# Tokens and their forms moved 96 bytes from the weight rings, and a causal mask read as a repeated view

## The chip, the cores and the metric

The kernel runs on one core of a Trainium2 chip. The metric is the device time of one execution in microseconds (us), here as the median of several runs. The engines are TensorE (PE, whose weight loads the profile lists as PEld), VectorE (DVE), ScalarE (ACT), GpSimd (POOL) and SyncE (SP), which issues most DMAs.

## What is computed

A decoder trunk of two layers for 512 tokens of width 1024, in float32 inputs and outputs. Each layer is a feed-forward block, a token mixer with four memory heads beside it, and another feed-forward block, each followed by a layer norm over a scaled residual. The mixer of layer 0 is latent attention (MLA), that of layer 1 sparse attention (NSA), whose keys and values come from the tokens after layer 0.

```python
def swiglu(x, w_gu, w_down):
    g, u = jnp.split(x @ w_gu, 2, axis=-1)
    return (jax.nn.silu(g) * u) @ w_down

for layer in range(DEPTH):                                  # DEPTH = 2
    x = layer_norm(DN_ALPHA * x + 0.5 * swiglu(x, ffn_w_gu[layer, 0], ffn_w_down[layer, 0]), ...)
    if layer < N_A_LAYERS:
        o_tok, q_mem = mla_mix(x, ...)                      # 12 heads, causal
    else:
        o_tok, q_mem = nsa_mix(x, ...)                      # compressed, selected and window keys, causal
    o_mem = memory_attention(q_mem, mem, w_mem_kv[layer])
    x = layer_norm(DN_ALPHA * x + jnp.concatenate([o_tok, o_mem], -1) @ w_out[layer], ...)
    x = layer_norm(DN_ALPHA * x + 0.5 * swiglu(x, ffn_w_gu[layer, 1], ffn_w_down[layer, 1]), ...)
    if layer == N_A_LAYERS - 1:
        shared = nsa_shared_kv(x, ...)
```

The hidden width is 2816, that is 22 blocks of 128.

## The kernel before

**Products in three parts.** Every operand of a large product is kept as two float32r tiles, a rounded part (hi) and the rest (lo), and a product is hi·hi + hi·lo + lo·hi. `split` makes the two: ScalarE rounds (L198), VectorE subtracts (L199).

**Weights.** A fixed list, `_unit_order`, names every weight unit of [128, 1024] floats in the order of use. `prep` loads a unit by a DMA on SP's queue into one of four `wraw` buffers and splits it into a pair `whi`, `wlo`. The pairs lie in a ring of three (`wring`) and, inside the feed-forward stages, also in an extension of four (`W.extra`, the pool `wx`). `ahead` runs up to four units before the use.

**Feed-forward.** The gate and up products have the weights stationary and the tokens streamed, feature-major. Of the 22 blocks some ("s") are computed directly by `feature_major` (L352, L354 and L357: whi with xhi, whi with xlo, wlo with xhi), the others ("d") by a scheme with seven quarter products in place of eight, `seven`, whose quarters stream 256 columns on L365, L366 and L369:

```python
        for k in range(4):
            ks = slice(off + k * P, off + (k + 1) * P)
            nc.tensor.matmul(ps, lhsT=hi[:, ks], rhs=xh[:, k], start=k == 0, stop=False)
            nc.tensor.matmul(ps, lhsT=hi[:, ks], rhs=xl[:, k], start=False, stop=False)
        for k in range(4):
            ks = slice(off + k * P, off + (k + 1) * P)
            nc.tensor.matmul(ps, lhsT=lo[:, ks], rhs=xh[:, k], start=False, stop=k == 3)
```

Here `xh`, `xl` are either cut views of the token tiles `xhi`, `xlo` ([128, 8, 512]) or combinations of their quarters, the forms `t` ([128, 4, 256] each), which `token_forms` makes once for each block from plain copies `b`. The down product and the output product of the mixer have the hidden tiles (`hhi`, `hlo`) or the mixed heads (`mix`) stationary and 512 columns of weights streamed: `prod`, L400 to L405.

**Other products named below.** The gate and memory-query projection of layer 1 (`gates_qmem`, by `mm3`, L344 to L346) keeps token tiles stationary, for each of four token tiles, and streams 292 columns of weights for each of eight k; three of these chunks lie one behind the other in a unit, at 0, 1168 and 2336 bytes. The compressed keys (also `mm3`) have 64 stationary columns (`zh`) under 256 streamed ones. In the NSA heads a causal mask is added to the scores by a bf16 matmul of the identity with a mask (L1137); there the mask stands twice, for selected and window keys, in 256 columns.

**Memory.** SBUF is handed out from both ends. On the left stand, in order: 4 KiB of descriptors and 128 bytes of small constants, the pool `const` (`cst` [128, 416] float32 and `cbf` [128, 384] bfloat16, 2432 bytes of a partition), `wraw`, `wring`, and then pools that come and go by stage. A feed-forward stage opens (`open_f`) `xp` (residual x0 to x3, norm gains `g`, `b`, and xhi, xlo), then `wx`, then `sm` and `fm` (the forms). Between the feed-forward stages this room holds the heads' tiles, in layer 1 the keys `ke`, `ko` and values first, then queries, `ptc` (transposed block scores) and scores. `hhi`, `hlo`, `mix` and `zh` come from the right end. There a 96-byte tile `rest` stands in the pool of statistics. All the tiles that matmuls read start on a multiple of 64 bytes.

**Order.** Each engine runs its instructions in order; SP's queue too. A tile that lies on room of an older tile waits until that one's last reader is done. After a mixer, `out_proj` reloads the residual tiles x0 to x3 that were spilled to HBM (L1213) and runs the output product; `residual` (L308) adds a tile's product, `norm_tile` norms it.

Of the kernel before, what the change touches and what calls it, by code (L numbers as in the profile page):

```python
# [9 lines left out]
F32 = mybir.dt.float32  # L10
F32R = mybir.dt.float32r
BF16 = mybir.dt.bfloat16
# [5 lines left out]
P = 128  # L18
# [12 lines left out]
NRAW, NRING, NEXTRA = 4, 3, 4  # L31
# [72 lines left out]
def tile_trunk(ctx: ExitStack, tc, a: dict, out):  # L104
    nc = tc.nc
    order = _unit_order()

    const = ctx.enter_context(tc.tile_pool(name="const", bufs=1))
# [8 lines left out]
    class W:  # L117
        pos = 0
        done = 0
        scope = None  # L120
# [84 lines left out]
    def zero(t):  # L205
        nc.vector.memset(t.bitcast(F32), 0.0)

    cst = const.tile([P, 416], F32, name="cst")
    nc.gpsimd.dma_start(cst[:, 0:400], a["cst"])
    ident = cst[:, 0:128]  # L210
    valid = cst[:, 384:385]
    cbf = const.tile([P, 384], BF16, name="cbf")
    identb = cbf[:, 0:128]
    maskb = cbf[:, 128:256]
    maskb2 = cbf[:, 128:384]
    mhalf = cst[:, 385:387]

    class F:
# [22 lines left out]
    def stat(tag, bufs):  # L241

        return small.tile([P, 2, 4], F32, tag=tag, name=tag, bufs=bufs)
# [7 lines left out]
    def s2tile():  # L251
        return PS.left.tile([P, 1024], F32, tag="s2", name="s2", bufs=2)

    def s1tile():
        return PS.left.tile([P, 512], F32, tag="s1", name="s1")
# [6 lines left out]

    def open_f(scope):
        F.st = ExitStack()
        F.xp = F.st.enter_context(tc.tile_pool(name=f"xp{scope}", bufs=1, reuse_waits="tile"))
        W.extra = F.st.enter_context(tc.tile_pool(name=f"wx{scope}", bufs=NEXTRA, reuse_waits="tile"))
        F.sm = F.st.enter_context(tc.tile_pool(name=f"sm{scope}", bufs=2, reuse_waits="tile"))
        F.x = [F.xp.tile([P, D], F32, name=f"x{t}") for t in range(NT)]
        F.bk = 0
        W.scope = scope  # L270
        W.count = 0
        F.fst = ExitStack()
        F.fm = F.fst.enter_context(tc.tile_pool(name=f"fm{scope}", bufs=1, reuse_waits="tile"))
# [291 lines left out]
    def memory_pool():  # L565
        M.st, M.mp = right_pool("memp")
# [529 lines left out]
    def nsa_heads(gt, qf):  # L1096
# [18 lines left out]
        def weigh(rs, gi):  # L1115

            nc.vector.scalar_tensor_tensor(rs, rs, 1e-30, gi, op0=ALU.max, op1=ALU.mult)
            nc.vector.reciprocal(rs, rs)

        def head(u):  # L1120
            nm, rs = (stat(e, 3).rearrange("p a (b r) -> p (a b) r", r=2) for e in ("nm", "rs"))
            pp = hp.tile([P, 2560], F32, tag="p", name="pp", bufs=5)
            pbuf[u] = pp
            pr, par = divmod(u, 2)
            h = pr + 6 * par
            qt = F.qx[pr % 2][par]
            kt = (S.ke, S.ko)[par]
            for i in (3, 2, 1, 0):
                s = s1tile() if i == 1 else s2tile()
                q = slice(i * P, (i + 1) * P)  # L1130
                n = (i + 1) * P
                for c0 in range(0, 2 * n, 512):
                    c1 = min(c0 + 512, 2 * n)
                    for x in range(2):
                        nc.tensor.matmul(s[:, c0:c1], lhsT=qt[:, x, q], rhs=kt[:, x, c0:c1],  # L1135
                                         start=x == 0, stop=x == 1 and c1 < 2 * n)
                nc.tensor.matmul(s[:, 2 * n - 256:2 * n], lhsT=identb, rhs=maskb2, start=False, stop=True)  # L1137
                sv = s[:, 0:2 * n].rearrange("p (b r k) -> p r b k", r=2, k=P)
                po = pp[:, 2 * P_OFF[i]:2 * P_OFF[i] + 2 * n].rearrange("p (r b k) -> p r b k", r=2, k=P)
                nc.vector.tensor_reduce(nm[:, i], sv, axis=AX.XY, op=ALU.max, negate=True)  # L1140
                for r in range(2):
                    nc.scalar.activation(po[:, r], sv[:, r], AF.Exp,
                                         bias=nm[:, i, r:r + 1], accum_out=rs[:, i, r:r + 1])
                if i in (2, 0):
                    weigh(rs[:, i // 2 * 2:i // 2 * 2 + 2], gt[:, i // 2 * 2:i // 2 * 2 + 2, 3 * h + 1:3 * h + 3])
                    for ii in (i // 2 * 2, i // 2 * 2 + 1):
                        n = (ii + 1) * P
                        po = pp[:, 2 * P_OFF[ii]:2 * P_OFF[ii] + 2 * n].rearrange("p (r k) -> p r k", r=2)
                        nc.gpsimd.tensor_tensor(po, po, rs[:, ii, :, None].to_broadcast([P, 2, n]), op=ALU.mult)
                yield  # L1150
# [24 lines left out]
        def scores():  # L1175
            for u in range(HEADS):
                yield from head(u)
# [50 lines left out]
    for side in ("left", "right"):  # L1228
        psum_pool(side, "f0")
    open_f(0)  # L1230
    new_xt()
    new_blocks()
# [16 lines left out]
                prep()  # L1249
    sst.close()  # L1250
    nc.vector.tensor_copy(cbf[:, 0:256], cst[:, 0:256])
    nc.vector.tensor_copy(cbf[:, 256:384], cst[:, 128:256])
    memory_pool()

    def load_x():
# [17 lines left out]
    ast.close()  # L1273
    shared_pool()
    open_f(1)
    out_proj(0)
    mst.close()
# [18 lines left out]
    ast.close()  # L1296
    S.st.close()
    open_f(2)
    out_proj(1)
    mst.close()  # L1300
# [154 lines left out]
```

## Time and profile before

| | us |
|---|---|
| median of 3 runs | 1921.31 (1921.25 to 1922.46) |
| the profiled execution | 1921.12 |
| its span in the profile | 1919.2 |
| PE busy, PEld busy | 1888.3, 1686.0 |
| DVE, ACT, POOL busy | 1470.2, 870.1, 164.4 |

The profile records one execution. Busy time counts the stretches in which an engine has at least one instruction under way; matmuls overlap, so the distance between the starts of two that follow each other tells more than their durations. Times in its rows are us from the start of the span, mean durations in groups are ns. L198 is line 198 of the kernel.

### The profile page before, as it was taken

To read this page: it belongs to the slowest core of one execution; us is meant where nothing else is said; L and a number is where in the kernel's file an instruction comes from. 1 tells how busy PE (TensorE), PEld (TensorE's weight loads), DVE (VectorE), ACT (ScalarE), POOL (GpSimd) and SP (SyncE) were. 2 spreads that over 40 slices of the span, in tenths; PEclk is the share of its full clock that TensorE was granted. 3 is DMA by queue.
4 is the path that set the end of the run, shared out by engine and by line. 5 is a ranking of instruction groups with operands and counts; after the bars stand their busy time and mean duration, and the time that the engine had idled before them with its cause. 6 is when DMAs were issued, how large, how long until landed. Compare 5 with 4: busy or idle time off the path is not lost.

```text
span 1919.2 us, 31480 instructions
## 1 busy us (share of the span) xinstructions
PE 1888.3 (98%) x12560; PEld 1686.0 (88%) x12560; DVE 1470.2 (77%) x2363; ACT 870.1 (45%) x1435; POOL 164.4 (9%) x185
## 2 busy tenths in 40 slices
PE   9999999999999999999999999999999999999998
PEld 8999999886679999999989999998856689999997
DVE  7788788757658779778787987977477477887886
ACT  5344344446545335334653433444466344434432
POOL 0000000025400000000100000001255200000000
PEclk9999999999999999999999999999999999999999
DMA  6333334530133234234333323334321324323322
GB/s 235 110 110 101 119 99 147 175 100 34 45 121 129 81 100 132 77 100 143 120 112 110 121 87 100 121 105 160 110 45 27 101 75 132 101 87 110 111 79 75
DMA packets 59715, 203.88 MB, mean 106 GB/s; under 512 B 6945, under 2 KB 7217, under 8 KB 59569
## 3 DMA queue, kind: packets, MB, share of 16 engines
q1 hardware_dynamic: 57136, 194.70, 31.2%
q0 software_dynamic: 2432, 7.17, 1.3%
q8 instruction: 99, 1.62, 0.4%
q14 instruction: 48, 0.39, 0.1%
HBM read 188.21 MB, written 7.34 MB: 102 GB/s over the span
## 4 chain that ended last, share of the span: by engine, by line
PE 91%; DVE 3%; ACT 2%; issue 1%; POOL 1%; DMA 1%; POOLq 0%; DVEq 0%; ACTq 0%
PE bank L366 14%; PE bank L369 13%; PE bank L365 13%; PE bank L404 4%; PE bank L402 4%; PE bank L401 4%; PE bank L400 4%; PE bank L403 4%; PE bank L405 4%; PE bank L357 3%; PE bank L354 3%; PE bank L352 3%; PE o L633 3%; PE tb L605 3%; PE s L1135 1%; PE bank L346 1%
## 5 line engine op out<-in xcount | busy, mean ns | idle before, releaser
L198 ACT CAST whi<-wraw 128x1024 fp32r<-128x1024 f32 (+3 forms) x479 | 463.0, 974 | 593.5 <-PE bank L405 255.9
L199 DVE TENSOR_TENSOR wlo<-wraw,whi 128x1024 fp32r<-128x1024 f32 (+3 forms) x479 | 536.5, 1126 | 138.5 <-ACT whi L198 129.8
L366 PE MATMUL bank<-t,whi 128*128 128x256 f32 x1232 | 309.1, 284 | 0.0
L365 PE MATMUL bank<-t,whi 128*128 128x256 f32 x1232 | 309.0, 283 | 0.0
L366 PEld LDWEIGHTS bank<-t,whi 128*128 128x128 f32 x1232 | 237.0, 192 | 0.0
L365 PEld LDWEIGHTS bank<-t,whi 128*128 128x128 f32 x1232 | 236.8, 192 | 0.0
L366 PE MATMUL bank<-xlo,whi 128*128 128x256 f32 x924 | 231.8, 284 | 0.0
L365 PE MATMUL bank<-xhi,whi 128*128 128x256 f32 x924 | 231.7, 283 | 0.0
L369 PE MATMUL bank<-t,wlo 128*128 128x256 f32 x1232 | 198.3, 284 | 0.0
L366 PEld LDWEIGHTS bank<-xlo,whi 128*128 128x128 f32 x924 | 177.7, 192 | 0.7
L365 PEld LDWEIGHTS bank<-xhi,whi 128*128 128x128 f32 x924 | 177.4, 192 | 0.7
L369 PEld LDWEIGHTS bank<-t,wlo 128*128 128x128 f32 x1232 | 170.1, 192 | 0.0
L308 DVE SCALAR_TENSOR_TENSOR x<-x,bank 128x512 f32<-128x512 f32 x176 | 112.6, 682 | 68.2 <-PE bank L404 65.4
L369 PE MATMUL bank<-xhi,wlo 128*128 128x256 f32 x924 | 148.7, 284 | 0.0
L403 PE MATMUL bank<-wlo,hhi 128*128 128x512 f32 x336 | 131.3, 391 | 0.0
L401 PE MATMUL bank<-whi,hhi 128*128 128x512 f32 x336 | 131.2, 390 | 0.0
L404 PE MATMUL bank<-whi,hlo 128*128 128x512 f32 x336 | 131.1, 390 | 0.0
L405 PE MATMUL bank<-whi,hlo 128*128 128x512 f32 x336 | 131.0, 390 | 0.0
L400 PE MATMUL bank<-whi,hhi 128*128 128x512 f32 x336 | 130.9, 390 | 0.0
L402 PE MATMUL bank<-wlo,hhi 128*128 128x512 f32 x336 | 130.9, 390 | 0.0
L352 PE MATMUL bank<-xhi,whi 128*128 128x256 f32 (+1 forms) x472 | 129.5, 305 | 1.3 <-ACT xhi L198 1.3
L354 PE MATMUL bank<-xlo,whi 128*128 128x256 f32 (+1 forms) x472 | 129.4, 305 | 0.9 <-DVE xlo L199 0.9
(331 smaller groups left out, 3532.9 us busy)
## 6 DMA issues: line engine op xcount, KB each, us to landing
wraw<-in_gu SPq DMA_DIRECT2D x175, 512.0 KB, 3.4
wraw<-in_dn SPq DMA_DIRECT2D x88, 512.0 KB, 3.9
wraw<-in_wo SPq DMA_DIRECT2D x16, 512.0 KB, 3.6
wraw<-in_wm SPq DMA_DIRECT2D x8, 512.0 KB, 4.3
x_dram<-x SPq DMA_DIRECT2D x8, 512.0 KB, 2.9
x<-x_dram SPq DMA_DIRECT2D x8, 512.0 KB, 4.1
wraw<-in_w SPq DMA_DIRECT2D x8, 512.0 KB, 4.4
wraw<-in_wq SPq DMA_DIRECT2D x6, 512.0 KB, 3.7
```

The costliest lines, as they stand in the source:

```text
L198: nc.scalar.copy(hi, src)
L199: eng.tensor_tensor(lo, src, hi.bitcast(F32), op=ALU.subtract)
L352: nc.tensor.matmul(ps[:, c0:c1], lhsT=hi[:, k * P:(k + 1) * P], rhs=F.xhi[:, k, c0:c1], start=k == 0, stop=False)
L365: nc.tensor.matmul(ps, lhsT=hi[:, ks], rhs=xh[:, k], start=k == 0, stop=False)
L366: nc.tensor.matmul(ps, lhsT=hi[:, ks], rhs=xl[:, k], start=False, stop=False)
L369: nc.tensor.matmul(ps, lhsT=lo[:, ks], rhs=xh[:, k], start=False, stop=k == 3)
L400: nc.tensor.matmul(p0, lhsT=ahi, rhs=hi[:, 0:512], start=first, stop=False)
L401: nc.tensor.matmul(p1, lhsT=ahi, rhs=hi[:, 512:1024], start=first, stop=False)
L402: nc.tensor.matmul(p0, lhsT=ahi, rhs=lo[:, 0:512], start=False, stop=False)
L403: nc.tensor.matmul(p1, lhsT=ahi, rhs=lo[:, 512:1024], start=False, stop=False)
L404: nc.tensor.matmul(p0, lhsT=alo, rhs=hi[:, 0:512], start=False, stop=last)
L405: nc.tensor.matmul(p1, lhsT=alo, rhs=hi[:, 512:1024], start=False, stop=last)
```

## The change

It shortens `cst` to the 400 columns that are used, and drops the second copy of the mask in `cbf` with the copy that filled it. `const` is then 2112 bytes of a partition, 320 less, and `wraw` and `wring` start 320 bytes earlier. The mask matmul of the NSA heads reads the one mask through a view that repeats it. In a feed-forward stage `wx` is opened ahead of `xp`, and `xp` begins with a tile of 24 floats, 96 bytes, that nothing reads or writes. So both weight rings stay on the 64-byte grid, and x0 to x3, g, b, xhi, xlo, the forms and their copies start 32 bytes off it.

```diff
-    cst = const.tile([P, 416], F32, name="cst")
+    cst = const.tile([P, 400], F32, name="cst")
     nc.gpsimd.dma_start(cst[:, 0:400], a["cst"])
...
-    cbf = const.tile([P, 384], BF16, name="cbf")
+    cbf = const.tile([P, 256], BF16, name="cbf")
     identb = cbf[:, 0:128]
     maskb = cbf[:, 128:256]
-    maskb2 = cbf[:, 128:384]
...
     def open_f(scope):
         F.st = ExitStack()
+        W.extra = F.st.enter_context(tc.tile_pool(name=f"wx{scope}", bufs=NEXTRA, reuse_waits="tile"))
         F.xp = F.st.enter_context(tc.tile_pool(name=f"xp{scope}", bufs=1, reuse_waits="tile"))
-        W.extra = F.st.enter_context(tc.tile_pool(name=f"wx{scope}", bufs=NEXTRA, reuse_waits="tile"))
+        F.xp.tile([P, 24], F32, name="offset")
...
-                nc.tensor.matmul(s[:, 2 * n - 256:2 * n], lhsT=identb, rhs=maskb2, start=False, stop=True)
+                nc.tensor.matmul(s[:, 2 * n - 256:2 * n], lhsT=identb, rhs=maskb[:, None, :].to_broadcast([P, 2, P]), start=False, stop=True)
...
     nc.vector.tensor_copy(cbf[:, 0:256], cst[:, 0:256])
-    nc.vector.tensor_copy(cbf[:, 256:384], cst[:, 128:256])
```

## Rows read from the trace of the kernel before

**Rows 1.** Busy time of each engine; granted PE clock in 40 slices (tenths).

```profile
PE 1888.3 (98%) x12560; PEld 1686.0 (88%) x12560; DVE 1470.2 (77%) x2363; ACT 870.1 (45%) x1435; POOL 164.4 (9%) x185
...
PEclk9999999999999999999999999999999999999999
```

**Rows 2.** The chain that ended last, by engine.

```profile
PE 91%; DVE 3%; ACT 2%; issue 1%; POOL 1%; DMA 1%; POOLq 0%; DVEq 0%; ACTq 0%
```

**Rows 3.** Groups by form: count, busy us, mean ns.

```profile
L365 PE MATMUL bank<-t,whi 128*128 128x256 f32 x1232 | 309.0, 283 | 0.0
...
L365 PE MATMUL bank<-xhi,whi 128*128 128x256 f32 x924 | 231.7, 283 | 0.0
...
L400 PE MATMUL bank<-whi,hhi 128*128 128x512 f32 x336 | 130.9, 390 | 0.0
...
L352 PE MATMUL bank<-xhi,whi 128*128 128x256 f32 x400 | 99.8, 286 | 1.3 <-ACT xhi L198 1.3
```

**Rows 4.** Timeline of PE, quarter products: start us, duration us; twelve starts apart.

```profile
200.57 0.28 PE L365 MATMUL bank<-t,whi 128*128 128x256 f32 x1
...
202.01 0.28 PE L365 MATMUL bank<-t,whi 128*128 128x256 f32 x1
```

**Rows 5.** Timeline of PE, output product of layer 0; twelve starts apart.

```profile
546.43 0.39 PE L400 MATMUL bank<-whi,mix 128*128 128x512 f32 x1
...
549.15 0.39 PE L400 MATMUL bank<-whi,mix 128*128 128x512 f32 x1
```

**Rows 6.** Timeline of PE, compressed keys; twelve starts apart.

```profile
965.97 0.28 PE L344 MATMUL bank<-whi,zh 128*64 128x256 f32 x1
...
967.33 0.28 PE L344 MATMUL bank<-whi,zh 128*64 128x256 f32 x1
```

**Rows 7.** Timeline of PE, gate projection of layer 1, second token tile.

```profile
1331.60 0.30 PE L344 MATMUL bank<-whi,xhi 128*128 128x292 f32 x1
...
1332.40 0.30 PE L344 MATMUL bank<-whi,xhi 128*128 128x292 f32 x1
...
1332.81 0.29 PE L344 MATMUL bank<-whi,xhi 128*128 128x292 f32 x1
...
1333.20 0.30 PE L344 MATMUL bank<-whi,xhi 128*128 128x292 f32 x1
...
1334.81 0.30 PE L344 MATMUL bank<-whi,xhi 128*128 128x292 f32 x1
```

**Rows 8.** Timeline of PE, start of layer 0's second feed-forward block.

```profile
585.73 0.28 PE L352 MATMUL bank<-xhi,whi 128*128 128x256 f32 x1
...
586.44 1.12 PE L357 MATMUL bank<-xhi,wlo 128*128 128x256 f32 x8
587.40 0.28 PE L352 MATMUL bank<-xhi,whi 128*128 128x256 f32 x1
...
588.00 0.28 PE L354 MATMUL bank<-xlo,whi 128*128 128x256 f32 x1
```

**Rows 9.** Layer 1's heads end: SP, PE, DVE timelines; a window's busy, clock, DMA.

```profile
1488.86 9.61 SPq L1213 DMA_DIRECT2D x<-x_dram  x4
1528.21 0.33 SPq L129 DMA_DIRECT2D wraw<-in_wo  x1
...
1524.22 1.13 PE L1164 MATMUL o<-ptc,svc 128*128 128x512 f32 x2
...
1539.79 0.69 DVE L308 SCALAR_TENSOR_TENSOR x<-x,bank 128x512 f32<-128x512 f32 x1 [1.73 <-PE bank L404]
...
1520.00:1540.00 20.00, 19.99 (x89) 14.47 (x88) 9.86 (x10) 8.52 (x10) 1.14 (x2) 1.00 0.64 203
```

**Rows 10.** Mask matmuls and second mask copy: duration ns min/median/max.

```profile
L1137 PE MATMUL s<-cbf x48: 272/284/287, 1390.5 to 1497.3; 128*128 128x256 bf16 x48
...
L1252 DVE CAST cbf<-cst x1: 219/219/219, 6.8 to 6.8; 128x128 bf16<-128x128 f32 x1
```

## The prediction

> **What bounds the kernel now.** The page's busy row comes first: PE is busy for 98% of the span, at a granted clock of nine tenths or more in every slice, and the chain that ended last is 91% PE [rows 1, 2]. So the time is a count of matmuls times the distance from one start to the next, and a change of layout matters where it changes that distance. This is not the mean in the groups (283 ns and more), which overlaps the next matmul; it comes from the starts in the timeline.
>
> The groups by form give the counts [rows 3]: with the token tiles and their forms (xhi, xlo, t) as the streamed operand there are 1232 + 924 = 2156 matmuls of 256 columns on L365, as many on each of L366 and L369, and 400 on each of L352, L354 and L357: 6468 + 1200 = 7668. The timeline shows twelve of them in 202.01 - 200.57 = 1.44 us, 120.0 ns each [rows 4]. At 2.4 GHz, the level that the clock stands at here, 256 columns take 106.7 ns: each loses 13.3 ns. The output and down projections, 512 columns with the weights streamed, lose the same: 549.15 - 546.43 = 2.72 us for twelve, 226.7 ns against 213.3 [rows 5]. Where only 64 stationary columns are loaded, twelve streams of 256 take 1.36 us, 113.3 ns each: half the loss [rows 6]. So the loss goes with the load of the next weights that runs under the stream; the two meet somewhere. This is what 32 bytes could change: 7668 x 120.0 ns = 920 us, 48% of the span, of which 102 us are loss.
>
> The Trainium skill says on the page TensorE: Matmul & The Clock Gate (Part 2, step by step) that PE has two independent SBUF read ports, so that loading the next weights takes no read bandwidth from the running matmul. The trace does not bear this out here: 120.0 ns with 128 stationary columns, 113.3 with 64.
>
> **The change part by part.** *Tokens 32 bytes off the grid.* Before, streamed and stationary operands all start on the 64-byte grid. After, const is 320 bytes shorter, so the rings move by 320 and stay on the grid, and xhi, xlo and t stand 96 bytes further than they, off it. No row shows a 256-column stream so placed. Two rows come near.
>
> The first is the gate projection in layer 1: 292 columns of streamed weights, in chunks of 292 floats, so that of each three chunks the first starts on the grid, the second 16 bytes off and the third 32 off, under stationary tokens that stay on it. One chunk is three matmuls from one L344 start to the next [rows 7]. The third chunk takes 1332.81 - 1332.40 = 0.41 us, the next, on the grid again, 0.39; starts are read to 10 ns, so this is 136.7 against 130.0 ns with 5 of doubt. The whole token tile, eight chunks of mixed place, takes 1334.81 - 1331.60 = 3.21 us for 24 matmuls, 133.8 ns: a loss of 12.1 over 121.7. A stream that doesn't always start in step thus loses 12.1 instead of 13.3, which is -1.2 ns.
>
> The second is what the 256-column matmuls themselves do just after a disturbance: from 585.73 to 586.44 six take 0.71 us, 118.3 ns each, and a microsecond on (587.40 to 588.00) five take 0.60, 120.0 again [rows 8]. So 120.0 is no floor; it is a state that the stream falls into, with both operands on the grid. One that starts half a grid step later need not fall into it: -1.7 ns.
>
> I take the first, since it includes shifted operands in a steady stream: 7668 x 1.2 = -9.2 us. Bounds: below, the loss halves as with 64 stationary columns, -6.7 ns or -51 us; above, the costliest chunk (136.7 ns, loss 15.0) gives +1.7 ns or +13 us, and the step from rows 6 to rows 4, taken once more, +6.7 ns or +51.
>
> The Trainium skill has SBUF lines of 16 bytes (SBUF — State Buffer, Door 1, the note on cachelines). By that rule 32 bytes are two whole lines, and the term would be 0 instead of -9.2 us. The trace doesn't decide it: the means of chunks in different places differ by hardly more than their starts are read to.
>
> *Rings against the tiles that stay.* hhi, hlo and mix stay where they are, the rings move by 320 bytes; both remain on the 64-byte grid. Stationary tiles at steps of 256 bytes show one distance throughout [rows 6]. I take 0; 1 ns either way on the 6 x 336 matmuls of the down projection would be 2 us [rows 3].
>
> *Pools exchanged.* With the ring extension ahead of the tokens, tiles cover other old tiles at a change of stage. In layer 1, x0 to x3 lay over ke and ko, and their four loads went out from 1488.86 to 1498.47, while the heads still ran. After, x0 and x1 lie over ptc, which L1164 reads last at 1524.22 for 1.1 us, so that all four (2 MB) go out at about 1525.4. SP works in order; behind them stand the last wo load (1528.21) and the next gate weights. Their issue isn't later, since the wo load waits for its buffer anyway; its landing is. At the 203 GB/s of that stretch 2 MB are 10 us and its own 0.5 MB 2.5, so it lands by 1538, with its cast and difference still to come, and PE wants it for the last six products of tile 0, 1.4 us before the residual at 1539.79 [rows 9]. PE, and behind it the norm of tile 0, would be late by about 2 us. If the transfers overlap better it is 0; if the two gain loads (1 MB more, 5 us) go first it is 7. In layer 0 the x tiles move the other way, from tiles that the last value products read to score tiles that come free before. I take +1 for both.
>
> *Mask and copy.* The second mask copy, 219 ns on DVE, goes [rows 10]: at most 0.2 us at the start, taken as 0, since the splits of the first tokens stand before it. The 48 mask matmuls of L1137 read as many columns as before, 284 ns each, through a repeated view. No row shows a repeated stream; at half the rate it would cost 48 x 0.107 = 5 us, and a gain is excluded, because the columns are as many. Taken as 0, since the quarters of xhi and xlo are read through cut views at the same 120.0 ns as whole tiles.
>
> *VectorE, ScalarE and DMA on tiles 32 bytes off.* No row shows a large one. DVE is 77% and ACT 45% busy under PE's 98% [rows 1], which is the cover. Without it, the most that could come is a second helping of all that PE idles now, 1919.2 - 1888.3 = 31 us. Taken as 0.
>
> **Sum.** The profiled execution took 1921.12 us, 1.92 more than its span and 0.2 under the median of 1921.31. 1921.1 - 9.2 + 1 = **1913 us**. 0.2% (3.8 us) is about what a measurement of this kernel can tell from no change; that is 0.5 ns per token matmul.
>
> **The rivals.** (a) *The place doesn't matter*: the loss follows the number of columns loaded, not where they lie. For it: rows 4 to 6 go by columns. Against it: the return from 118.3 to 120.0, with nothing changed but the phase. Only the exchanged pools remain: 1922, between 1918 and 1925. (b) *Off the grid is worse*: the chunk that starts on the grid is the shortest of rows 7, the one 32 off the longest. At the loss of that chunk, 15.0 ns, it is +1.7 ns on all 7668, +13 us, 1935 with the pools. It decides as soon as the distance on L365 is above 120.5 ns. Against it: the 256-column stream loses more on the grid than the mean of rows 7, whatever its place. (c) *The step breaks altogether*: 117 ns down to the 113.3 of rows 6, -23 to -51 us, 1871 to 1899. Against it: a microsecond after the disturbance the matmuls were back at 120.0. (d) *The offset doesn't take*, because a pool rounds its tiles up to the grid: then it is (a), within whose share it lies.
>
> **How the numbers follow.** The mild gain has 0.33 (its own range 1903 to 1917), (b) 0.30, (a) 0.27, (c) 0.10. So faster by over 0.2% is 0.43, within 0.2% 0.27, slower 0.30. The range may leave out at most 2 in 10: most of (c) below, and above the part of (b) that comes nearer to +6.7 ns than to +1.7: 1890 to 1939.
>
> **What would show it.** The distance of starts on L365, L366 and L369 in the middle of a group: 118 to 119.5 ns for the forecast, 120.0 for (a), above 120.5 for (b), 117 or below for (c). L400 to L405 should stay at 226.7 and L1137 at 284. In layer 1 the x loads should go out near 1525 with a wait of 0 to 2 us before tile 0 ends. The prediction is wrong if the token distance moves by more than 2 ns either way, or if it stays and the time still moves.

## The result, and the profile after

The kernel after takes 1932.92 us, median of four runs (1931.55 to 1934.23), beside 1921.28 (1920.36 to 1922.46) for the kernel before, measured beside it: ratio 1.0061, 95% interval 1.0046 to 1.0076. It is slower by 0.6%, 11.6 us. The time lies inside the predicted range (1890 to 1939), on the other side of before than the forecast of 1913. The profiled execution took 1931.55, 1.95 more than its span.

The page's busy row and its chain of work that ended last, after:

```profile
span 1929.6 us, 31480 instructions
...
PE 1901.5 (99%) x12560; PEld 1685.6 (87%) x12560; DVE 1471.3 (76%) x2362; ACT 870.4 (45%) x1435; POOL 164.2 (9%) x185
...
PE 93%; DVE 3%; ACT 2%; POOL 1%; issue 1%; DMA 0%; POOLq 0%; DVEq 0%; ACTq 0%
```

The span is 10.4 us longer, and PE is busy for 13.2 us more [rows 1] with the same 12560 matmuls. PE's idle time fell, from 30.9 to 28.1 us. So no new wait is to be sought: some matmuls follow each other more slowly. Which ones, the groups by form tell (count, then busy us and mean ns; they answer to [rows 3]):

```profile
L366 PE MATMUL bank<-t,whi 128*128 128x256 f32 x1232 | 309.7, 285 | 0.0
L365 PE MATMUL bank<-t,whi 128*128 128x256 f32 x1232 | 308.4, 280 | 0.0
...
L369 PE MATMUL bank<-t,wlo 128*128 128x256 f32 x1232 | 197.2, 281 | 0.0
...
L404 PE MATMUL bank<-whi,hlo 128*128 128x512 f32 x336 | 133.7, 398 | 0.0
...
L400 PE MATMUL bank<-whi,hhi 128*128 128x512 f32 x336 | 133.4, 397 | 0.0
L403 PE MATMUL bank<-wlo,hhi 128*128 128x512 f32 x336 | 132.4, 394 | 0.0
```

The token streams changed in both directions: two of the three lines are shorter (280 and 281 ns, from 283 and 284), one is longer (285, from 284). The down projection's six lines changed in one: 390 or 391 ns before, 394 to 398 now. The timeline of the output product of layer 0, the stretch of [rows 5], shows the distance (start us, duration us):

```profile
546.27 0.39 PE L400 MATMUL bank<-whi,mix 128*128 128x512 f32 x1
546.50 0.40 PE L401 MATMUL bank<-whi,mix 128*128 128x512 f32 x1
546.74 0.39 PE L402 MATMUL bank<-wlo,mix 128*128 128x512 f32 x1
...
549.07 0.39 PE L400 MATMUL bank<-whi,mix 128*128 128x512 f32 x1
```

Twelve now take 549.07 - 546.27 = 2.80 us, 233.3 ns each, where they took 226.7; read to the nanosecond, 231 and 236 alternate. All starts of the two traces, added up by line from one start to the next, give the account:

```
start to next start, us           before    after    median ns before -> after
L365, L366, L369 (6468 matmuls)   776.03   776.17    120, 120, 120 -> 117, 124, 120
L352, L354, L357, 256 col (1200)  149.41   148.84    120 -> 120, 119, 119
L400 to L405, hhi and hlo (2016)  459.13   471.25    227 -> 231 or 236
```

The last row is +12.1 us, 6.0 ns on each of 2016 matmuls: the whole loss, and more than the 10.4 us of the span. The quarters of the tokens, which the change set out to move, add 0.1. All the rest together is 1.9 us shorter. (The sums hold the pauses too, so that their means stand a little above the medians.)

### The profile page after: what moved, and what is told of

It is laid out like the page before. It is cut to its first block, busy times and chain, and to the rows that moved or that the text cites. A ratio compares the mean times of both kernels' runs of the same rounds, so it can differ in the third digit from the quotient of the medians.

```text
span 1929.6 us, 31480 instructions
## 1 busy us (share of the span) xinstructions
PE 1901.5 (99%) x12560; PEld 1685.6 (87%) x12560; DVE 1471.3 (76%) x2362; ACT 870.4 (45%) x1435; POOL 164.2 (9%) x185
## 4 chain that ended last, share of the span: by engine, by line
PE 93%; DVE 3%; ACT 2%; POOL 1%; issue 1%; DMA 0%; POOLq 0%; DVEq 0%; ACTq 0%
PE bank L366 14%; PE bank L369 13%; PE bank L365 13%; PE bank L404 5%; PE bank L402 5%; PE bank L400 5%; PE bank L401 5%; PE bank L403 5%; PE bank L405 4%; PE bank L357 3%; PE bank L354 3%; PE bank L352 3%; PE o L633 3%; PE tb L605 3%; PE s L1135 1%; PE bank L346 1%
## 5 line engine op out<-in xcount | busy, mean ns | idle before, releaser
L366 PE MATMUL bank<-t,whi 128*128 128x256 f32 x1232 | 309.7, 285 | 0.0
L365 PE MATMUL bank<-t,whi 128*128 128x256 f32 x1232 | 308.4, 280 | 0.0
L366 PE MATMUL bank<-xlo,whi 128*128 128x256 f32 x924 | 232.3, 285 | 0.0
L365 PEld LDWEIGHTS bank<-t,whi 128*128 128x128 f32 x1232 | 232.3, 189 | 0.0
L365 PE MATMUL bank<-xhi,whi 128*128 128x256 f32 x924 | 231.3, 280 | 0.0
L366 PEld LDWEIGHTS bank<-t,whi 128*128 128x128 f32 x1232 | 231.2, 188 | 0.0
L369 PE MATMUL bank<-t,wlo 128*128 128x256 f32 x1232 | 197.2, 281 | 0.0
L365 PEld LDWEIGHTS bank<-xhi,whi 128*128 128x128 f32 x924 | 174.2, 189 | 0.8
L366 PEld LDWEIGHTS bank<-xlo,whi 128*128 128x128 f32 x924 | 173.4, 188 | 0.7
L369 PEld LDWEIGHTS bank<-t,wlo 128*128 128x128 f32 x1232 | 169.9, 189 | 0.0
L369 PE MATMUL bank<-xhi,wlo 128*128 128x256 f32 x924 | 147.9, 281 | 0.0
L400 PE MATMUL bank<-whi,hhi 128*128 128x512 f32 x336 | 133.4, 397 | 0.0
L405 PE MATMUL bank<-whi,hlo 128*128 128x512 f32 x336 | 132.2, 393 | 0.0
```

Source lines behind the costliest of these rows:

```text
L400: nc.tensor.matmul(p0, lhsT=ahi, rhs=hi[:, 0:512], start=first, stop=False)
L405: nc.tensor.matmul(p1, lhsT=alo, rhs=hi[:, 512:1024], start=False, stop=last)
```

## The experiments

**Theory 1**: the loss comes from the rings. They moved 320 bytes, and the down and output products stream them over hidden tiles that stayed. **Theory 2**: the tokens off the 64-byte grid cost it. **Theory 3**: the exchanged pools or the repeated view. **Theory 4**: it is the rings' own place in SBUF that counts, not that against the tiles they meet. In all edits below, a pool's size sets where the next one begins.

**The rings put back, the tokens left at 96.** The unused zeros between the mask and the last 16 columns of `cst` are left out too, so that `const` is 512 bytes shorter than before in place of 320.

```diff
-    cst = const.tile([P, 400], F32, name="cst")
-    nc.gpsimd.dma_start(cst[:, 0:400], a["cst"])
+    cst = const.tile([P, 352], F32, name="cst")
+    nc.gpsimd.dma_start(cst[:, 0:256], a["cst"][:, 0:256])
+    nc.gpsimd.dma_start(cst[:, 256:272], a["cst"][:, 384:400])
```

> The kernel after, with only the constant tile cut further (the unused zeros of the constants left out), so that the weight rings stand in the same phase to hhi and hlo as before, and the tokens still 96 bytes beyond the rings. Theory 1 (the loss is in the output and down projections, because the rings moved against the hidden tiles): back to about 1920 us (1917 to 1923), L400 to L405 at 226.7 ns from start to start again, the token streams of 256 columns at a mean of 120 ns. Rival theory 2 (the tokens off the grid cost it): stays at about 1933 us.

Measured: 1920.16 us beside 1919.86 for before, ratio 0.9999 (0.9990 to 1.0007). L400 to L405 stand at 227 ns again (459.35 us in all). The tokens still go by line, now at 123, 118 and 119.5 on L365, L366 and L369 (776.20 us).

**The rings and the tokens moved together.** The kernel before with the constants cut as in the change, and with its repeated mask view; the pools in their old order, no offset.

```diff
-    cst = const.tile([P, 416], F32, name="cst")
+    cst = const.tile([P, 400], F32, name="cst")
...
-    cbf = const.tile([P, 384], BF16, name="cbf")
+    cbf = const.tile([P, 256], BF16, name="cbf")
```

> The kernel before with only the constants cut (mask as a repeated view, no second mask copy): the rings and the tokens move together by 320 bytes against hhi and hlo; no pools exchanged, no tokens moved against the rings. Theory 1: about 1933 us (1930 to 1936), L400 to L405 at 233 to 234 ns, the token streams locked at 120.0. Theory 2: about 1921 us.

Measured: 1932.72, ratio 1.0069 (1.0055 to 1.0083), the whole loss without the offset or the exchange. Groups by form of the two runs, first the one with the rings put back, then this one (a line has a number one higher in the first than in the kernel after, and one lower in the second):

```profile
L404 PE MATMUL bank<-wlo,hhi 128*128 128x512 f32 x336 | 130.9, 390 | 0.0
L405 PE MATMUL bank<-whi,hlo 128*128 128x512 f32 x336 | 130.9, 390 | 0.0
```

```profile
L365 PE MATMUL bank<-t,whi 128*128 128x256 f32 x1232 | 308.9, 283 | 0.0
...
L402 PE MATMUL bank<-wlo,hhi 128*128 128x512 f32 x336 | 133.8, 398 | 0.0
L400 PE MATMUL bank<-whi,hhi 128*128 128x512 f32 x336 | 133.7, 398 | 0.0
```

In the second the tokens stand at 283 as before, with a median distance of 120 on all three lines, and the down projection has the 398 of the change. Theory 1 stands, theory 2 falls.

**The pools exchanged, nothing else** (with the repeated mask view; `cst` and `cbf` keep their sizes).

```diff
+        W.extra = F.st.enter_context(tc.tile_pool(name=f"wx{scope}", bufs=NEXTRA, reuse_waits="tile"))
         F.xp = F.st.enter_context(tc.tile_pool(name=f"xp{scope}", bufs=1, reuse_waits="tile"))
-        W.extra = F.st.enter_context(tc.tile_pool(name=f"wx{scope}", bufs=NEXTRA, reuse_waits="tile"))
```

> The kernel before with the two pools exchanged and the mask as a repeated view, every size kept, so that all stands on the same places to 512 bytes. Theory 1: 1918 to 1921 us, what the exchange gives by itself (PE idle 28 us instead of 31). Rival theory 3 (the exchange of pools or the repeated view costs it): 1925 us or more.

Measured: 1918.65, ratio 0.9995 (0.9986 to 1.0004): no difference that can be told, and no loss. Theory 3 falls.

**The hidden tiles moved with the rings.** The kernel after, with `const` cut to 1600 bytes and the unused tile at the right end widened, so that hhi, hlo and mix also stand 320 bytes lower. The rings are then 832 bytes lower than before, that is 320 and another 512.

```diff
-    small.tile([P, 24], F32, name="rest")
+    small.tile([P, 104], F32, name="rest")
```

> The kernel after with hhi, hlo and mix moved by the same 320 bytes, so that the rings stand to them as before, but neither on the 512-byte places of before; the tokens still 96 bytes beyond the rings. Theory 1 with the relative place as what counts: about 1920 us, L400 to L405 at 226.7 ns. Rival theory 4 (the absolute place counts): stays at about 1933 us, 233 to 234 ns. Theory 2: about 1933 us with L400 to L405 at 226.7.

Measured: 1919.46, ratio 0.9997 (0.9989 to 1.0006), L400 to L405 at 227. What counts is the difference between where the streamed operand starts and where the stationary one does. Theory 4 falls.

**Every distance by itself.** A kernel of matmuls alone, executed once: for each of 32 tiles that start 0, 16, ... 496 bytes beyond the stationary one, it runs 96 streams of 512 columns, and later 96 of 256.

```diff
+    def narrow(o, n):
+        m = mv[o][:, o // 4:o // 4 + 256]
+        for i in range(n):
+            nc.tensor.matmul(b[2][:, 0:256], lhsT=st[:, (i % 8) * P:(i % 8 + 1) * P], rhs=m, start=i == 0, stop=i == n - 1)
```

> Not the reference's computation but the disputed distance by itself: one stationary tile of eight 128 x 128 weights (taken in turn, loaded anew for each matmul) and streams of 512 and then of 256 columns, 96 matmuls each, from 32 tiles that start 0, 16, 32, ... 496 bytes beyond the stationary tile, modulo 512. Theory 1: at 0 the distance from start to start is 226.7 ns for 512 columns and 120.0 for 256; at 192 it is 233 to 234 for 512 columns; 256 columns keep 120.0 at 96. Theory 2 (off the 64-byte grid costs, on it not): 226.7 and 120.0 at all multiples of 64, more in between. If the place doesn't matter by itself, all 64 groups show 226.7 and 120.0, and the kernel's loss needs something beside the place, its other tiles or its other engines.

Measured, as windows inside the groups of 256 columns at 0, 96, 112 and 192 bytes (the count in 10 us stands behind PE's busy time, then the granted clock):

```profile
729.00:739.00 10.00, 10.00 (x86) 1.00 0.01 2
797.00:807.00 10.00, 10.00 (x85) 1.00 0.00 0
808.50:818.50 10.00, 10.00 (x90) 1.00 0.00 0
865.00:875.00 10.00, 10.00 (x90) 1.00 0.01 2
```

With PE busy and the full clock throughout, 90 matmuls go where 85 or 86 went. The mean distances from the starts, in ns; from 256 bytes on the same values return to 0.1 ns:

```
bytes     0    16    32    48    64    80    96   112   128   144   160   176   192   208   224   240
256 col 120.0 118.7 116.7 118.3 117.8 120.0 120.0 113.3 118.7 118.6 117.3 119.2 113.3 119.2 118.4 117.1
512 col 226.7 231.7 233.3 233.3 228.9 231.1 233.4 231.0 232.5 233.3 234.2 231.1 233.3 234.7 233.3 226.7
```

From this table the change can be read. The rings went from 0 to -320 bytes against hhi, hlo and mix, which is 192 modulo 256: 226.7 to 233.3 for the 512 columns. The tokens went from 0 to 96: 120.0 to 120.0, one of the few places that give nothing. The 64-byte grid means nothing here: 192 is on it and costs the wide streams 6.6 ns, 240 is off it and costs none.

**Other offsets in the kernel.** Three kernels follow from the table; the first two move the rings by 256 bytes, which keeps them in phase, that is at the same distance from hhi and hlo modulo 256.

```diff
-    cst = const.tile([P, 400], F32, name="cst")
+    cst = const.tile([P, 416], F32, name="cst")
...
-        F.xp.tile([P, 24], F32, name="offset")
+        F.xp.tile([P, 48], F32, name="offset")
```

> The kernel after with an offset of 192 bytes in place of 96, and the constant tile at its old 416 columns, so that the rings move by 256 bytes instead of 320: in phase with hhi and hlo by the sweep, which repeats after 256 bytes. By the sweep's rows the token streams of 256 columns go from 120.0 to 113.3 ns, L400 to L405 stand at 226.7, the few token streams of 512 columns at 233.3: 7668 x 6.7 = 51 us less and 216 x 6.6 = 1.4 more, some 1870 us (1866 to 1876 if no other engine becomes the bound). If the sweep doesn't carry over to the kernel, because there the streams alternate between tiles and other engines read: 1917 to 1922.

The same with `[P, 8]`:

> As the run with 192 bytes, but 32 bytes of offset: tokens off the 64-byte grid, rings in phase with hhi and hlo. By the sweep 116.7 ns for the token streams of 256 columns and 233 for those of 512: 7668 x 3.3 = 25 us less, 1.4 more, some 1896 us. If it is the 64-byte grid that counts (96 and 32 alike), 1920 us as with 96.

The kernel after with `[P, 48]` as its only edit:

> The kernel after with nothing changed but the offset, 192 bytes in place of 96; the rings still 320 bytes from where they stood. The two terms by the sweep: tokens at 113.3 (51 us less), L400 to L405 at 233 to 234 (12 us more): some 1882 us (1878 to 1888).

Measured, beside 1919.80 for before: 1898.43 with 192 bytes (ratio 0.9889, 0.9874 to 0.9903), 1894.42 with 32 (0.9866, 0.9852 to 0.9881), 1900.26 with 192 and the rings out of phase (0.9897, 0.9880 to 0.9913). At 32 bytes the quarters stand at 116.7 ns as in the table, and the time is within 2 us of what was worked out. At 192 they do not stand at 113.3: with the rings in phase the mean is 117.7, with the rings out of phase 115.6. Each of the 20 unbroken groups of quarters (168 to 420 matmuls long) keeps one distance: with the rings in phase one group has 113.3 and 19 have 117.8, with the rings out of phase ten have 113.3 or 113.4 and ten 117.8. So the two expectations of 192 bytes were 28 and 18 us too low: the table's 113.3 there isn't the only state.

**The kernel's own order, from eight starts.** Quarter products by themselves at ten offsets, each eight times, after a matmul of another width; executed once.

```diff
+    for o in steps:
+        for r in range(8):
+            for q in range(4):
+                quarter(b[q % 2][:, 0:256], q % 2 * 512, *xs[o])
+            kick(72 + 16 * r)
```

> Not the reference's computation, but the kernel's own order of quarter products by themselves: for ten offsets (0, 32, 64, 96, 112, 128, 160, 192, 224, 240 bytes) eight runs of 48 streams of 256 columns, before each of which a matmul of another width (72 to 184 columns) shifts the moment at which the run starts; then the same streams with a new weight tile for every matmul, as in the first sweep. The kernel with 192 bytes showed 117.7 ns where the first sweep showed 113.3. If the order of the kernel (each weight tile used for two streams running) makes the difference, the quarters at 192 show 117 to 118 whatever the start, and the second half 113.3. If the moment of the start chooses between two states, both halves at 192 show 113.3 in some of the eight runs and 117 to 118 in others. At 0 and 96 120.0, at 32 116.7 in either case.

Measured, the mean distance in each of the eight runs of 48, the first three distances left out (the second half, with a new weight tile for every matmul, shows the same within 0.1 ns but for the first start at 0 bytes: the kernel begins with it, and its first distances are above 200 ns):

```
  0 bytes: 123.7 119.8 119.8 120.0 119.8 119.7 119.7 119.7
 32 bytes: 116.6 116.7 117.8 117.8 117.7 117.8 117.8 116.7
 64 bytes: 113.3 117.8 117.8 117.8 117.8 117.8 117.8 117.8
 96 bytes: 120.0 120.0 119.9 120.0 120.0 119.9 119.9 120.0
112 bytes: 114.3 113.8 114.2 114.3 114.2 113.8 113.8 114.3
192 bytes: 113.4 117.8 117.8 113.4 117.8 113.4 117.8 117.8
```

The moment of the start chooses the state at 192 (113.4 or 117.8), and the stream keeps it. It does so at 32 bytes too (116.7 or 117.8), and of the offsets not shown at 128 (118.6 to 120.0) and 160 (117.2 to 118.8): in these rows the first sweep's table has one state of several. The kernel with 32 bytes had 116.6 or 116.7 in all 20 groups. At 112 every start leads to 113.3 within a dozen matmuls. The order of weights makes no difference.

**112 bytes in the kernel.** Tiles start on multiples of 32 bytes, so xhi and xlo become two views, 16 bytes into one tile, and so do four of the eight forms. The other four share buffers with the raw blocks and stand at 32 bytes.

```diff
-        F.xhi = F.xp.tile([P, NKT, T], F32R, tag="xhi", name="xhi")
-        F.xlo = F.xp.tile([P, NKT, T], F32R, tag="xlo", name="xlo")
+        xt = F.xp.tile([P, 2 * NKT * T + 8], F32R, tag="xt", name="xt")
+        F.xhi, F.xlo = (xt[:, 4 + e * NKT * T:4 + (e + 1) * NKT * T].rearrange("p (k q) -> p k q", k=NKT)
+                        for e in range(2))
...
+        tt = F.fm.tile([P, 4 * 1024 + 8], F32R, tag="t", name="t")
+        own = {tag: tt[:, 4 + j * 1024:4 + (j + 1) * 1024].rearrange("p (k q) -> p k q", k=4)
+               for j, tag in enumerate(("t1h", "t2h", "t2l", "t4h"))}
```

> The rings in phase with hhi and hlo, and the tokens where the second sweep showed 113.3 ns from every start: xhi and xlo as views of one tile, 112 bytes beyond the rings modulo 256; of the token forms t those four that share no buffer with the raw blocks (t1h, t2h, t2l, t4h) at 112 too, the other four (t1l, t3h, t3l, t4l) at 32. By the sweeps: 2772 quarter matmuls of xhi and xlo, 1200 of the feature-major products and 7 of 12 of the 3696 on t at 113.3 (6128 x 6.7 = 41 us less), the other 1540 at 116.7 (5 us less), the 216 token streams of 512 columns at 231 (1 more): some 1875 us (1870 to 1882), against 1894 with all at 32 and 1898 with all at 192. If the streams at two places disturb each other, or the joined tiles bring waits, it stays at 1885 or above.

Measured: 1887.16 us beside 1920.40, ratio 0.9826 (0.9809 to 0.9842), the fastest of all, 1.7% under the kernel before. Its groups by form (L373 is L369 of the kernel before, L408 is L400):

```profile
L373 PE MATMUL bank<-t,wlo 128*128 128x256 f32 x1232 | 192.8, 278 | 0.0
L373 PE MATMUL bank<-xt,wlo 128*128 128x256 f32 x924 | 143.2, 276 | 0.0
...
L408 PE MATMUL bank<-whi,hhi 128*128 128x512 f32 x336 | 130.8, 390 | 0.0
```

The quarters of xhi and xlo stand at a median of 113 to 114 ns (mean 115.0), those of the forms at a mean of 116.5, where a mixture of 113.3 and 116.7 would be 114.7. The sums of all 6468 fell by 26.5 us, those of the 1200 by 4.9. It stays at 1887, above the 1870 to 1882 expected. For the quarters some 38 us less had been expected, so that 11.5 are missing. The distances quarter by quarter, 924 matmuls each, in the order of `seven` (x with the halves of depth and tokens that it takes), tell where:

```
quarter          x(0,0)  x(1,0)    t4      t1      t2      t3    x(1,1)
hi / lo, bytes  112/112 112/112  112/32  112/32 112/112   32/32 112/112
mean, ns         114.0   113.3   116.9   117.8   114.8   116.7   117.8
```

Quarters at one place reach that place's distance once the stream has settled: x(1,0) has 113.3, t3 116.7. In t4 and t1 the streams alternate between two places, and they hold neither's distance: a mixture would be 114.4 ns, which is 5.4 us less than measured. The other 6.1 us lie in t2, x(1,1) and x(0,0), which stand wholly at 112 but come after a stream at another place or one not yet settled; the dozen matmuls that a start at 112 can need to settle are a whole quarter. The joined tiles bring no new long wait: PE's longest for them is 1.6 us, as for xhi in the kernel after.

## Why the prediction was wrong

**The bound** was read rightly: PE's matmuls, one start after the other. The loss came as a longer distance, with PE's idle time lower than before. But "the loss goes with the load of the next weights", read from 64 columns at 113.3 ns against 128 at 120.0, does not hold as a rule of columns. The same stretch of compressed keys after the change (answering to [rows 6]):

```profile
965.97 0.28 PE L345 MATMUL bank<-wlo,zh 128*64 128x256 f32 x1
...
967.40 0.28 PE L345 MATMUL bank<-wlo,zh 128*64 128x256 f32 x1
```

Twelve starts now take 1.43 us, 119.2 ns each, with the same 64 columns; the rings moved against `zh` as against hhi. In the run with the rings put back they stand at a median of 113 again. And 128 columns at 113.3 exist, in the sweep at 112 bytes.

**"Rings against the tiles that stay ... I take 0"** is the step that failed. It measured +12.1 us, six times the 2 us that the step held possible. Two reasons stood behind the 0. "Both remain on the 64-byte grid" assumed that the grid counts; the sweep shows a pattern of 16-byte steps that repeats after 256. And [rows 6] showed stationary tiles in steps of 256 bytes at one distance throughout: a step of exactly one period comes back to the same place, so this row could not have shown a difference. A shift of 320 bytes takes the same row to 119 ns. The term should have had the bounds given to the tokens. At the up to 6.7 ns a matmul of the step from rows 6 to rows 4, 2016 matmuls are 13.5 us.

**"Tokens 32 bytes off the grid": -9.2 us** measured +0.1 on the quarters. The evidence for it was sound in kind: 120.0 was a state, not a floor [rows 8], and a shifted stream did leave it, to 117, 124 and 120 in turn. But the mean at 96 bytes is 120.0 again, as the sweep shows too. At 32 bytes the same step would have been worth 25 us, at 112 more. The chunks of [rows 7] couldn't say so: each lay at another distance only for three matmuls, and a stream in the sweeps can need a dozen to settle. The case that the prediction itself named as wrong came about: the token distance stays, and the time still moves.

**Rival (b)** gave 1935, close to the time, by a mechanism that did not occur: its sign, L365 above 120.5 ns, was not there (117, and 120.0 as the mean of the three lines), and the run with the tokens off the grid and the rings in phase is at 0.9999. So it is luck that 1932.92 lies inside 1890 to 1939: the range reached so far up for dearer tokens, and what paid was the term put at 0. **Rival (a)** was right on the tokens' sum and wrong that place doesn't matter. **Rival (c)** does not happen at 96 bytes; at 112 the quarters do reach 113.3. **Rival (d)** falls: the offset took, since 32 and 96 bytes differ by 26 us (1894.42 and 1920.16, both with the rings in phase).

**"Pools exchanged: +1".** The loads of x0 to x3 were moved as described. The timelines of SP's queue, of PE at the last reader of the old tiles and of DVE at the residual of tile 0, after (answering to [rows 9]; the span is some 6.5 us behind there):

```profile
1531.87 1.75 SPq L1213 DMA_DIRECT2D x<-x_dram  x4
1534.65 0.33 SPq L129 DMA_DIRECT2D wraw<-in_wo  x1
...
1530.67 1.12 PE L1164 MATMUL o<-ptc,svc 128*128 128x512 f32 x2
...
1546.57 0.69 DVE L308 SCALAR_TENSOR_TENSOR x<-x,bank 128x512 f32<-128x512 f32 x1 [0.32 <-PE bank L404]
```

All four go out 0.08 us after L1164's last matmul ends by the profile, 43 us later than the first did before. Hardly anything was late by it: the residual follows 15.90 us after the start of L1164, where it was 15.57, and the run with the exchange alone is at 0.9995. The term is 0, at the low end that the step gave.

**"Mask and copy": 0** held: L1137 has a median of 283 ns [rows 10], and the second copy is gone. **VectorE, ScalarE and DMA on tiles off the grid: 0** held too: DVE is busy for 1471.3 us against 1470.2.

**Two rules that the prediction cited.** By the Trainium skill's page SBUF — State Buffer (Door 1, the note on cachelines of 16 bytes) the token term would have been 0. Measured was 0.1; but the same rule gives 0 for 32 and for 112 bytes too, where the first sweep shows 3.3 and 6.7 ns less. The distances change in 16-byte steps; that lines cause them no run here shows. By the Trainium skill's page TensorE: Matmul & The Clock Gate (Part 2, step by step) the weight load takes no read bandwidth from the running stream. The trace does not agree in effect: the sweep's distances differ by up to 6.7 ns for one and the same load, by nothing but the place of the stream against it. So the two affect each other; by what path, no run here shows.

## What to carry to other kernels

Where matmuls follow each other without a pause and each loads new weights, the place of the streamed operand against the stationary one, modulo 256 bytes, is a parameter: here it was worth up to 1.7% of the kernel's time, and cost 0.6%. Sweep it for the stream's own width, since the best place for 256 columns (112) is not that for 512 (0 or 240), and from several starts, since one start shows one state of several. Only float32r streams were swept here. A shift of one tile is a shift against every tile that meets it in any product: list all pairs before pricing one, and choose each pair's place. Keep operands that alternate in one product at one place. A row that shows "no difference" at one step says nothing of other steps.

## What the runs showed of the hardware

- The distance of 128 x 128 float32r matmuls at 2.4 GHz depends on the start of the stream less the start of the weights, with a period of 256 bytes: 113.3 to 120.0 ns for 256 columns, 226.7 to 234.7 for 512. Moving both operands alike, modulo 256, changed nothing (the tokens and the rings by 320 bytes: 120.0 ns; the hidden tiles by 320 and the rings by 832: 227).
- At 64 and 192 bytes a stream of 256 columns has two steady states, 113.3 and 117.8 ns, and the moment of its start decides which; at 32 bytes they are 116.7 and 117.8. A kernel at 192 bytes had 113.3 in one or in ten of its 20 groups of quarters, with nothing different but the rings' place against the tiles that stay.
- With 64 stationary columns the place counts as well: 113.3 ns at one, 119 at another.
- Distances of single matmuls can differ by 5 or 7 ns around a steady mean: 231 and 236 (mean 233.3), or 117, 124 and 120 (mean 120.0), by the program's lines.
